# The first strip of a decoder trunk: order of loads, transposes by pairs of blocks, order of splits, six idle products

## The chip, the cores and the metric

The kernel runs on one core of a Trainium2 chip. The metric is the device time of one execution in microseconds (us). The kernel before takes 2492.08 us (median of 3 runs, 2491.33 to 2492.79). Five engines work side by side, each through its own list of instructions, strictly in the order of that list: PE (TensorE: products and transposes), DVE (VectorE), ACT (ScalarE), POOL (GpSimd) and SP (SyncE), which here does nothing but issue DMAs. ACT and POOL issue some DMAs too. An instruction that waits for another engine or for a DMA holds up everything behind it in its own list.

## The reference, cut to what matters

```python
for i in range(DEPTH):                                   # DEPTH = 2, x is 256 x 2048, f32
    h = rms_norm(x, pre_mix_gain[i])
    m = hybrid_mixer(h, positions, w_in[i], ...)         # proj = h @ w_in, then heads, then @ w_out
    x = x + rms_norm(m, post_mix_gain[i])
    h = rms_norm(x, pre_ffn_gain[i])
    f = (silu(h @ w_ffn_gate[i]) * (h @ w_ffn_up[i])) @ w_ffn_down[i]
    x = x + rms_norm(f, post_ffn_gain[i])
    gate = sigmoid(rms_norm(x, ple_gain[i]) @ w_ple_gate[i])
    x = x + (p[i] @ w_ple_proj[i]) * gate
```

Only the very first product is touched: 512 columns of `h @ w_in[0]`, those of the keys and values. `rope` turns the keys afterwards with tables of cosines and sines, which the kernel works out once, at its start.

## The kernel before, in words

**Products.** Every f32 matrix product is made of three products of rounded parts: a factor is split into a high part (`fp32r`, a rounding copy on ACT) and a low part (the rest, a subtraction on DVE), and PE adds high x high, low x high and high x low. `part` (L225 to L234) issues these three for 128 rows of the weight and one token tile of 128 tokens.

**Strips.** `strip` computes 512 output columns for both token tiles, in 8 chunks of 256 weight rows. For each chunk `load_w` (L209) fetches 256 x 512 weights into a tile `wr` (a ring of 4, so a fetch waits until the low split four chunks earlier has read its buffer), makes the high part `wh` on ACT (L173) and the low part `wl` on DVE (L174); `wh` and `wl` are rings of 8, so a split waits until PE has done the chunk eight before. A chunk is 12 products on PE: 2 blocks of 128 rows x 2 token tiles x 3.

**The left factor.** x comes in as eight tiles of 128 tokens x 512 columns, `xr[t][c]`. PE needs it turned, so each 128x128 block is transposed (L188, with `ident`) into a PSUM tile `ms`; then it is multiplied with the norm's gain and split into two `ck` tiles, high and low. In the first strip of all, `load_x` (the argument `pre`) does this between the chunks. For the first 512 columns (`wide`) a token tile's four blocks are multiplied at once on DVE into a tile `nat` (L180), and then split by ACT (L173) and DVE (L174). For the other 1536 columns each block is done by itself: ACT multiplies and rounds (L199), then DVE multiplies and subtracts (L200).

**What sets the order.** The program is written in the order of the Python code, but a scheduler of the framework lists each engine's instructions; `tc.high_priority()` lets a part go ahead, and `behind(names)` keeps the instructions inside it after those that `marks` names. Behind the first strip the order is the same as in a normal strip.

**Other work at the start.** Five idle products of `ident` (L123, `WARM`), one transpose of the first gain rows (L125), `square_sum` of x on ACT (L169), and from the fifth chunk on `constants()`: five small DMAs of gain rows issued by ACT (L136, L138), their transposes on PE (L140, L141) and copies on DVE (L142, L143), and some fifty small DVE instructions, most of them for `rope`'s angles (L361 to L393), which end in the tables `rot` (L438). When the first strip is done, `done_kv` takes its result: DVE multiplies it with the tables (L447), POOL adds and subtracts the halves (L454), and seven chunks later in PE's list the rotated keys are transposed (L466).

Of the kernel before, what the change touches and what calls it, by code (L numbers as in the profile page):

```python
# [46 lines left out]
def decoder(ctx: ExitStack, tc: tile.TileContext, x, p, positions, w_in, attn_sinks,  # L47
# [54 lines left out]
    def nat(shape=(P, W), dt=F32):  # L102
        return np_.tile(list(shape), dt, tag="nat", name="nat")
# [18 lines left out]
    for i in range(WARM):  # L122
        T.matmul(busy[:, 0:P], ident, ident, start=True, stop=True)  # L123
    ps = bank()
    T.transpose(ps[:, 0:32], g0rows, ident[0:32, 0:32])  # L125
    S.preload_act_table(AF.Copy)
# [47 lines left out]
        v = V.tensor_tensor(lo, src, hi.bitcast(F32), op=ALU.subtract)  # L174
        return a, v

    def split_wide(ps, gcols, h, lo):

        g = nat((P, 4, P))
        V.tensor_tensor(g, ps, gcols.unsqueeze(2).to_broadcast([P, 4, P]), op=ALU.mult)  # L180
        marks["x"], _ = split(g, h, lo)

    def split_T(src_blocks, gcols, hl, t, kt0=0, wide=False):
# [10 lines left out]
        if wide:  # L194
            split_wide(ps, gcols, h, lo)
            return
        for b in range(n):
            g = gcols[:, b:b + 1]
            marks["x"] = S.activation(h[:, b], ps[:, b], AF.Copy, scale=g)  # L199
# [6 lines left out]
    def blocks4(a):  # L206
        return [a[:, b * P:(b + 1) * P] for b in range(4)]

    def load_w(w, c, col):  # L209

        raw = wpr.tile([P, 2, W], F32, tag="wr", name="wr")
        nc.sync.dma_start(raw, w[c * 2 * P:(c + 1) * 2 * P, col:col + W].rearrange(
            "(k p) n -> p k n", p=P))
        hi = wps.tile([P, 2, W], F32R, tag="wh", name="wh")
        lo = wps.tile([P, 2, W], F32R, tag="wl", name="wl")
        marks["hi"], marks["lo"] = split(raw, hi, lo)
        return hi, lo

    def strip(lhs, w, col, done, nch=8, row0=0, skew=0, psum=None, pre=None):

        ps = psum or [pacc.tile([P, W], F32, tag="acc", name=f"acc{t}") for t in range(NT)]
        ws = {}

        def part(t, c, lows=(0, 1)):
            hi, lo = ws[c]  # L225
            for k in range(2):
                kt = 2 * c + k
                xh, xl = (a[:, kt % 4, t * P:(t + 1) * P] for a in lhs[kt // 4])
                first, last = kt == 0, kt == 2 * nch - 1
                if 0 in lows:  # L230
                    T.matmul(ps[t], xh, hi[:, k], start=first, stop=False)  # L231
                    T.matmul(ps[t], xl, hi[:, k], start=False, stop=False)  # L232
                if 1 in lows:
                    marks[t, c] = T.matmul(ps[t], xh, lo[:, k], start=False, stop=last)  # L234

        for i in range(nch + skew):
            if pre:
                pre(i)
# [35 lines left out]
        later(wait, lambda: turn((0, 1)))  # L274
        later(wait + 1, lambda: turn((2, 3)))

    def next_in(t, c, xT, gcols, wide=False):
        split_T(blocks4(xr[t][c]), gcols[:, 4 * c:4 * c + 4], xT[c], t, wide=wide)

    def new_ss(name):  # L280
        return [sm.tile([P, 4], F32, name=f"{name}{t}") for t in range(NT)]
# [115 lines left out]
    ss = new_ss("ssx")  # L397
    xT = [new_ck() for c in range(4)]

    def load_x(i):  # L400
        if i % 2 == 0:
            c = i // 2
            for t in range(NT):
                nc.sync.dma_start(xr[t][c], x[0, t * P:(t + 1) * P, c * W:(c + 1) * W])
            with tc.high_priority(), behind((1, i - 2)) if c else nullcontext():
                for t in range(NT):
                    next_in(t, c, xT, gain_cols(0, 0, 16), wide=c == 0)

            def squares():
                with behind("x", "hi"):  # L410
                    for t in range(NT):
                        square_sum(xr[t][c], ss[t][:, c:c + 1])
            later(1 if c == 3 else 2, squares)
        if i == 0:
            def tables():
                with behind((1, 3), "hi", "lo"):
                    constants()
            later(4, tables)

    for l in range(DEPTH):  # L420

# [459 lines left out]
```

## Time and profile before

| | |
|---|---|
| runs, median of 3 | 2492.08 us (2491.33 to 2492.79) |
| profiled execution | 2494.41 us, of which its span (first to last instruction) is 2492.4 us |
| PE busy | 2473.4 us, 99% of the span |
| DVE busy | 1433.2 us, 58% |
| ACT busy | 1177.6 us, 47% |
| chain that ended last | PE 95%, DVE 1%, DMA 1%, ACT 1% |

The shares are over the whole program, which is almost all strips in their steady form. The change concerns its first 60 us, so what counts is who waits for whom there. A matmul's shown duration includes the run through the array; what one costs in a row of them is the distance of two starts.

### The profile page before, as it was taken

How to read it: one execution, taken by the hardware profiler on the slowest of the kernel's cores; microseconds unless marked ns; L12 is line 12 of the kernel's file. 1: busy time of each engine (PE TensorE's matmuls, PEld its weight loads, DVE VectorE, ACT ScalarE, POOL GpSimd, SP SyncE). 2: the span in 40 equal slices, each digit the busy share in tenths (PEclk: the TensorE clock that was granted, in tenths of full speed). 3: DMA queues.
4: the chain of work that ended last, by engine and by line, in shares of the span. 5: the costliest groups of instructions: out<-in, count | busy, mean ns of one | idle time of the engine just before them, and what ended most of it. 6: DMA issues, size and time to landing. Idle time of an engine off the chain costs nothing.

```text
span 2492.4 us, 30948 instructions
## 1 busy us (share of the span) xinstructions
PE 2473.4 (99%) x11725; PEld 2049.2 (82%) x11725; DVE 1433.2 (58%) x1805; ACT 1177.6 (47%) x1676; POOL 96.3 (4%) x209
## 2 busy tenths in 40 slices
PE   8999999999999999999999999999999999999999
PEld 7888887888888888887888888878888888888877
DVE  7676656544554455457567756565445545554574
ACT  6644346444434434446556443464444344344462
POOL 3100001000000000001010000010000000000010
PEclk9999999999999999999999999999999999999999
DMA  8445465666666666665564454656666666666653
GB/s 263 137 139 165 144 193 159 215 191 190 192 188 194 188 193 194 189 200 157 186 204 134 136 173 140 199 170 197 191 190 187 193 193 189 192 190 195 200 169 129
DMA packets 234260, 451.43 MB, mean 181 GB/s; under 512 B 14176, under 2 KB 15104, under 8 KB 234112
## 3 DMA queue, kind: packets, MB, share of 16 engines
q1 hardware_dynamic: 233808, 449.37, 59.3%
q8 instruction: 92, 1.51, 0.3%
q14 instruction: 56, 0.46, 0.1%
q10 hardware_dynamic: 240, 0.07, 0.0%
q0 software_dynamic: 64, 0.02, 0.0%
HBM read 447.31 MB, written 2.10 MB: 180 GB/s over the span
## 4 chain that ended last, share of the span: by engine, by line
PE 95%; DVE 1%; DMA 1%; ACT 1%; issue 0%; POOL 0%; SPq 0%; ACTq 0%; DVEq 0%; POOLq 0%
PE acc L231 29%; PE acc L234 29%; PE acc L232 29%; PE ms L188 2%; DMA wr<-in_w_in_dram 1%; PE ms L661 1%; PE ms L561 1%; DVE wl L174 1%; PE ms L510 0%; ACT wh L173 0%; PE ms L639 0%; ACT junk L169 0%; PE ms L676 0%; PE ms L231 0%; PE ms L234 0%
## 5 line engine op out<-in xcount | busy, mean ns | idle before, releaser
L174 DVE TENSOR_TENSOR wl<-wr,wh 128x1024 fp32r<-128x1024 f32 x840 | 1029.0, 1226 | 960.0 <-ACT wh L173 948.5
L173 ACT CAST wh<-wr 128x1024 fp32r<-128x1024 f32 x840 | 883.4, 1053 | 1158.6 <-PE acc L232 1105.4
L231 PE MATMUL acc<-wh,ck 128*128 128x512 f32 x3328 | 1310.2, 394 | 7.9 <-ACT ck L199 5.6
L232 PE MATMUL acc<-wh,ck 128*128 128x512 f32 x3328 | 1298.6, 390 | 0.9 <-DVE ck L200 0.8
L234 PE MATMUL acc<-wl,ck 128*128 128x512 f32 x3328 | 1299.3, 391 | 0.0
L231 PEld LDWEIGHTS acc<-wh,ck 128*128 128x128 f32 x3328 | 625.6, 188 | 138.4 <-ACT ck L199 10.5
L232 PEld LDWEIGHTS acc<-wh,ck 128*128 128x128 f32 x3328 | 626.2, 188 | 130.8 <-DVE ck L200 4.4
L234 PEld LDWEIGHTS acc<-wl,ck 128*128 128x128 f32 x3328 | 625.6, 188 | 130.7
L199 ACT ACTIVATE ck<-ms,gT 128x128 fp32r<-128x128 f32 x248 | 79.3, 369 | 36.6 <-DVE ck L200 28.6
L200 DVE SCALAR_TENSOR_TENSOR ck<-ms,gT,ck 128x128 fp32r<-128x128 f32 x248 | 76.0, 346 | 21.8 <-ACT ck L199 21.0
L159 POOL TENSOR_TENSOR tiny<-ssf 128x1 f32<-128x1 f32 x4 | 2.1, 536 | 1379.0 <-ACT junk L169 1378.7
L779 ACT ACTIVATE nat<-acc,ry 128x512 f32<-128x512 f32 x44 | 30.2, 686 | 10.7 <-PE acc L234 10.7
L805 DVE TENSOR_TENSOR macc<-acc,macc 128x512 f32<-128x512 f32 x48 | 33.0, 688 | 0.7
L169 ACT ACTIVATE junk<-x 128x512 f32<-128x512 f32 x48 | 30.3, 631 | 6.4 <-DVE x L266 4.1
L785 DVE SCALAR_TENSOR_TENSOR nat<-acc,ry,nat 128x512 f32<-128x512 f32 x44 | 32.4, 748 | 0.1
L661 PEld LDWEIGHTS ms<-q,k 128*128 128x128 f32 x256 | 30.7, 191 | 1.7 <-PE acc L232 0.8
L661 PE MATMUL ms<-q,k 128*128 128x64 f32 x256 | 30.5, 272 | 0.0
L174 DVE TENSOR_TENSOR ck<-ms,ck 128x512 fp32r<-128x512 f32 x44 | 30.1, 684 | 0.0
L188 PE MATMUL ms<-ident,x 128*128 128x128 f32 x192 | 27.8, 281 | 2.1 <-DVE x L838 1.4
L188 PEld LDWEIGHTS ms<-ident,x 128*128 128x128 f32 x192 | 22.8, 144 | 8.5 <-DVE x L838 2.6
L188 PEld LDWEIGHTS ms<-ident,nat 128*128 128x128 f32 x184 | 22.7, 139 | 6.4 <-DVE ck L200 0.4
L188 PE MATMUL ms<-ident,nat 128*128 128x128 f32 x184 | 28.0, 272 | 0.0
(187 smaller groups left out, 861.9 us busy)
## 6 DMA issues: line engine op xcount, KB each, us to landing
wr<-in_w_in_dram SPq DMA_DIRECT2D x176, 512.0 KB, 3.8
wr<-in_w_ffn_gate_dram SPq DMA_DIRECT2D x176, 512.0 KB, 3.7
wr<-in_w_ffn_up_dram SPq DMA_DIRECT2D x176, 512.0 KB, 3.7
wr<-in_w_ffn_down_dram SPq DMA_DIRECT2D x176, 512.0 KB, 3.7
wr<-in_w_out_dram SPq DMA_DIRECT2D x64, 512.0 KB, 4.2
wr<-in_w_ple_gate_dram SPq DMA_DIRECT2D x64, 512.0 KB, 4.3
wr<-in_w_ple_proj_dram SPq DMA_DIRECT2D x8, 512.0 KB, 4.1
x<-in_x_dram SPq DMA_DIRECT2D x8, 256.0 KB, 6.8
```

Source lines behind the costliest of these rows:

```text
L169: S.activation(j[:, 0:shape[1]], src, AF.Square, accum_out=acc)
L173: a = S.copy(hi, src)
L174: v = V.tensor_tensor(lo, src, hi.bitcast(F32), op=ALU.subtract)
L188: T.transpose(ps[:, b], blk, ident)
L199: marks["x"] = S.activation(h[:, b], ps[:, b], AF.Copy, scale=g)
L200: V.scalar_tensor_tensor(lo[:, b], ps[:, b], g, h[:, b].bitcast(F32), op0=ALU.mult, op1=ALU.subtract)
L231: T.matmul(ps[t], xh, hi[:, k], start=first, stop=False)
L232: T.matmul(ps[t], xl, hi[:, k], start=False, stop=False)
L234: marks[t, c] = T.matmul(ps[t], xh, lo[:, k], start=False, stop=last)
L661: T.matmul(pl[:, t * 4 + h].rearrange("p (b k) -> p b k", k=k), s.k[:, h, t * P:(t + 1) * P], up, start=True, stop=True)
L785: V.scalar_tensor_tensor(gate[t], ps, rx2(t)[:, 0:1], gate[t], op0=ALU.mult, op1=ALU.mult)
L805: V.tensor_tensor(m, ps, m, op=ALU.add)
```

## The change

x is loaded in the order of use: the first 512 columns in two halves of 256 for both token tiles, with the first weight chunk between the halves; the next weight chunks are fetched inside `load_x` too, one after each 512 columns of x (`raws`). x is turned by `split_pair`: two blocks of both token tiles into one PSUM tile, one multiplication with the gain for the 128x512 elements, one high and one low split, for all 2048 columns; one such pair belongs to each chunk. The first chunk's high weight split stands ahead of the first pair's work on ACT. Each chunk's weight splits stand behind the splits of its own pair, and the next pairs behind the chunk before. Six idle products (`HOLD`) stand behind the first pair's transposes. The squares are taken one chunk after their pair.

```diff
+HOLD = 6
+    def idle_products(n):
+        for i in range(n):
+            T.matmul(busy[:, 0:P], ident, ident, start=True, stop=True)
+    idle_products(WARM)
...
+    def split_pair(kt, hl, gcols):
+        ps = bank((P, 2, NT, P))
+        for b in range(2):
+            for t in range(NT):
+                c, at = divmod((kt + b) * P, W)
+                marks["turned", kt] = T.transpose(ps[:, b, t], xr[t][c][:, at:at + P], ident)
+        g = nat((P, 2, SEQ))
+        V.tensor_tensor(g, ps.rearrange("p b t n -> p b (t n)"),
+                        gcols[:, kt:kt + 2].unsqueeze(2).to_broadcast([P, 2, SEQ]), op=ALU.mult)
+        k = slice(kt % 4, kt % 4 + 2)
+        marks["xh", kt], marks["xl", kt] = split(g, hl[0][:, k], hl[1][:, k])
...
-                with behind("x") if pre and i == 0 else nullcontext():
-                    ws[i] = load_w(w, row0 // (2 * P) + i, col)
+                with behind(("xh", 2 * i), ("xl", 2 * i)) if pre else nullcontext():
+                    ws[i] = load_w(w, row0 // (2 * P) + i, col, *ready)
...
     def load_x(i):
-        if i % 2 == 0:
-            c = i // 2
-            for t in range(NT):
-                nc.sync.dma_start(xr[t][c], x[0, t * P:(t + 1) * P, c * W:(c + 1) * W])
-            with tc.high_priority(), behind((1, i - 2)) if c else nullcontext():
-                for t in range(NT):
-                    next_in(t, c, xT, gain_cols(0, 0, 16), wide=c == 0)
+        def cols(a, n):
+            c, at = divmod(a, W)
+            for t in range(NT):
+                nc.sync.dma_start(xr[t][c][:, at:at + n], x[0, t * P:(t + 1) * P, a:a + n])
+        def pair(n):
+            split_pair(2 * n, xT[n // 2], gain_cols(0, 0, 16))
+        if i == 0:
+            for c in range(4):
+                if c == 0:
+                    cols(0, 256)
+                    raws[0] = fetch_w(w_in[0], 0, 1024)
+                    cols(256, 256)
+                else:
+                    cols(c * W, W)
+                if c < 3:
+                    raws[c + 1] = fetch_w(w_in[0], c + 1, 1024)
+            with tc.high_priority():
+                hi = high(raws[0])
+                with behind("hi"):
+                    pair(0)
+                with behind(("turned", 0)):
+                    idle_products(HOLD)
+        pairs = {0: (1,), 1: (2, 3)}.get(i, (i + 2,))
+        with tc.high_priority(), behind((1, i - 1)) if i else nullcontext():
+            for n in pairs:
+                if n < 8:
+                    pair(n)
```

PE's list at the program's start, before. `x00_82` and `x10_86` are the first 512 columns of the two token tiles, `ms` PSUM tiles, `acc0` and `acc1` the strip's sums, `DMAHW1` and `DMAHW2` the arrival of the two x tiles.

```order
L123 MATMUL ms_100<-ident_90 128x128 x4
L125 MATMUL ms_106<-ident_90,g0rows_97 128x32 [waits DMAHW0_49]
L188 MATMUL ms_155<-ident_90,x00_82 128x128 [waits DMAHW1_49]
L188 MATMUL ms_155<-ident_90,x00_82 128x128 x3
L188 MATMUL ms_164<-ident_90,x10_86 128x128 [waits DMAHW2_49]
L188 MATMUL ms_164<-ident_90,x10_86 128x128 x3
L231 MATMUL acc0_151<-wh_175,ck_133 128x512 [waits Activation_49]
```

The same place now. `ms_173` is the first pair and `ms_188` the second; `DMAHW1` and `DMAHW2` are the first halves of the two x tiles, `DMAHW4` and `DMAHW5` the second halves, which are issued behind the first weight chunk (`DMAHW3`).

```order
L129 MATMUL ms_106<-ident_90,g0rows_97 128x32 [waits DMAHW0_49]
L187 MATMUL ms_173<-ident_90,x00_82 128x128 [waits DMAHW1_49]
L187 MATMUL ms_188<-ident_90,x00_82 128x128 [waits DMAHW4_49]
L187 MATMUL ms_188<-ident_90,x10_86 128x128 [waits DMAHW5_49]
L187 MATMUL ms_173<-ident_90,x10_86 128x128 [waits DMAHW2_49]
L187 MATMUL ms_188<-ident_90,x00_82 128x128
L187 MATMUL ms_173<-ident_90,x00_82 128x128
L187 MATMUL ms_188<-ident_90,x10_86 128x128
L187 MATMUL ms_173<-ident_90,x10_86 128x128
L126 MATMUL ms_100<-ident_90 128x128 x6
L250 MATMUL acc0_151<-wh_171,ck_133 128x512 [waits Activation_49]
```

The two pairs' transposes now alternate, and the second transpose in the list waits for the second half of an x tile; the six idle products and the strip's first product stand behind all eight.

ACT's list where the small DMAs of gain rows stand (`grows`, `lrows`), before:

```order
L199 ACTIVATE ck_135<-ms_215,gT_99 128x128 [waits PE_49]
L199 ACTIVATE ck_135<-ms_228,gT_99 128x128 [waits PE_49]
L136 DMA grows_110<-in_pre_ffn_gain_dram 32x128 [waits DMAHW2_49]
L136 DMA grows_110<-in_ple_gain_dram 32x128 [waits DMAHW3_49]
L136 DMA grows_110<-in_attn_out_gain_dram 16x128 [waits DMAHW4_49]
```

And now (`nat_254` and `nat_283` are the fifth and the sixth pair, `wh_422` the fifth chunk's high part):

```order
L173 ACTIVATE junk_276,ssx1_132<-x11_87 128x512 [waits DMAHW0_49,Activation_49]
L177 CAST ck_137<-nat_254 128x512 [waits DVE_49]
L140 DMA grows_110<-in_pre_ffn_gain_dram 32x128
L140 DMA grows_110<-in_ple_gain_dram 32x128 [waits DMAHW6_49]
L140 DMA grows_110<-in_attn_out_gain_dram 16x128 [waits DMAHW7_49]
L140 DMA grows_110<-in_hgrn_out_gain_dram 16x128 [waits DMAHW0_49]
L142 DMA lrows_111<-in_hgrn_lb_logits_dram 16x128 [waits DMAHW1_49]
L177 CAST ck_137<-nat_283 128x512 [waits DVE_49]
L225 CAST wh_422<-wr_420 128x1024
```

The five issues stood among the second 512 columns' activations; now they stand together behind the fifth pair's high split, and ahead of the sixth pair's and of the fifth chunk's weight split.

DVE's list around the copies of those rows (L146, L147), now; `wl_424` and `wl_455` are the fifth and the sixth chunk's low parts, `nat_416` the seventh pair.

```order
L178 TENSOR_TENSOR ck_138<-nat_283,ck_137 128x512 [waits Activation_49]
L235 TENSOR_TENSOR wl_424<-wr_420,wh_422 128x1024 [waits DMAHW1_49,Activation_49]
L189 TENSOR_TENSOR nat_416<-ms_411,gT_99 128x512 [waits PE_49]
L146 COPY gT_99<-ms_308 128x96 [waits PE_49]
L147 COPY lbl_112<-ms_308 128x16
L235 TENSOR_TENSOR wl_455<-wr_451,wh_453 128x1024 [waits DMAHW2_49,Activation_49]
```

Before, seven low splits stood ahead of the first of these copies; now five do. From there to the rotation of the keys (L447 before, L495 now) the same low splits and small instructions follow, in other places among each other: in both lists the rotation stands behind the 21st low split, and PE's transposes of the keys stand behind 180 products. Behind that place all lists read alike.

## Rows read from the trace of the kernel before

**Rows 1.** Waits of PE, 0 to 75 us: total us, times, longest.

```profile
PE acc L231 <- ACT wh L173: 2.4, 1, 2.4
PE acc L231 <- ACT ck L199: 1.7, 4, 0.7
PE ms L123 <- POOL ident masks.py:199: 1.6, 1, 1.6
PE ms L466 <- POOL nat L454: 1.3, 1, 1.3
```

**Rows 2.** Chain that ended last, 50 to 75 us: start us, us, what.

```profile
55.38 1.23 DVE wl L174
56.60 0.40 DVE rot L438 x3
57.00 0.72 DVE nat L447 x2
57.78 1.94 POOL nat L454 x2
59.77 0.44 PE ms L466 x2
60.20 0.23 PE acc L231
```

**Rows 3.** Timeline, 0 to 15 us: start us, us, engine, what, [idle before].

```profile
1.56 2.50 PE L123 MATMUL ms<-ident 128*128 128x128 f32 x10 [1.56 <-POOL ident masks.py:199]
4.24 1.97 PE L188 MATMUL ms<-ident,x 128*128 128x128 f32 x8
5.39 0.69 DVE L180 TENSOR_TENSOR nat<-ms,gT 128x512 f32<-128x512 f32 x1 [0.85 <-PE ms L188]
7.49 1.99 ACT L173 CAST wh<-wr 128x1024 fp32r<-128x1024 f32 x2
8.58 0.80 PE L231 MATMUL acc<-wh,ck 128*128 128x512 f32 x1 [2.38 <-ACT wh L173]
9.60 0.63 PE L231 MATMUL acc<-wh,ck 128*128 128x512 f32 x1
10.03 0.63 PE L232 MATMUL acc<-wh,ck 128*128 128x512 f32 x1
13.85 1.04 PE L188 MATMUL ms<-ident,x 128*128 128x128 f32 x8
14.64 0.47 PE L231 MATMUL acc<-wh,ck 128*128 128x512 f32 x1
```

**Rows 4.** DMA issues in 0.7:1.2, 1.2:1.68, 1.68:2.1 and 2.6:3.15, last column us to landing.

```profile
x<-in_x_dram SPq DMA_DIRECT2D x1, 256.0 KB, 2.8
x<-in_x_dram SPq DMA_DIRECT2D x1, 256.0 KB, 3.5
wr<-in_w_in_dram SPq DMA_DIRECT2D x1, 512.0 KB, 5.3
x<-in_x_dram SPq DMA_DIRECT2D x1, 256.0 KB, 6.3
```

**Rows 5.** Timeline of SP's issues and ACT's, 0 to 20 us.

```profile
0.79 0.86 SPq L404 DMA_DIRECT2D x<-in_x_dram  x2
1.70 0.94 SPq L212 DMA_DIRECT2D wr<-in_w_in_dram  x2
15.29 0.43 ACTq L136 DMA_DIRECT2D grows<-in_ple_gain_dram  x1
19.09 0.32 ACTq L138 DMA_DIRECT2D lrows<-in_hgrn_lb_logits_dram  x1
```

**Rows 6.** Busy by stretch: us, PE (x), PEld, DVE, ACT, POOL, granted clock, DMA share, GB/s.

```profile
8.60:14.00 5.40, 5.40 (x14) 4.15 (x15) 3.61 (x4) 4.10 (x7) 0.16 (x6) 1.00 1.03 378
5.39:26.60 21.21, 17.89 (x75) 14.02 (x74) 14.43 (x24) 14.88 (x30) 4.18 (x40) 1.00 0.88 310
26.60:57.70 31.10, 30.37 (x135) 23.86 (x134) 27.14 (x79) 21.81 (x39) 6.36 (x8) 1.00 0.81 253
```

**Rows 7.** Groups by form on DVE, 5.3 to 57.8 us: xcount | busy us, mean ns | idle before.

```profile
L174 DVE TENSOR_TENSOR wl<-wr,wh 128x1024 fp32r<-128x1024 f32 x22 | 26.7, 1220 | 5.1 <-ACT wh L173 5.1
L200 DVE SCALAR_TENSOR_TENSOR ck<-ms,gT,ck 128x128 fp32r<-128x128 f32 x24 | 7.3, 345 | 4.9 <-ACT ck L199 4.8
L180 DVE TENSOR_TENSOR nat<-ms,gT 128x512 f32<-128x512 f32 x2 | 1.4, 692 | 1.0 <-PE ms L188 1.0
L174 DVE TENSOR_TENSOR ck<-nat,ck 128x512 fp32r<-128x512 f32 x2 | 1.4, 686 | 0.1
```

**Rows 8.** Timeline of PE, 57 to 60.6 us.

```profile
57.66 0.39 PE L231 MATMUL acc<-wh,ck 128*128 128x512 f32 x1
57.89 0.39 PE L232 MATMUL acc<-wh,ck 128*128 128x512 f32 x1
58.11 0.39 PE L234 MATMUL acc<-wl,ck 128*128 128x512 f32 x1
59.77 0.44 PE L466 MATMUL ms<-ident,nat 128*128 128x128 f32 x2 [1.26 <-POOL nat L454]
```

**Rows 9.** DMA issues, 0 to 70 us: KB each, median us to landing.

```profile
wr<-in_w_in_dram SPq DMA_DIRECT2D x29, 512.0 KB, 4.9
g0rows<-in_pre_mix_gain_dram ACTq DMA_DIRECT2D x1, 16.0 KB, 2.5
grows<-in_pre_ffn_gain_dram ACTq DMA_DIRECT2D x1, 16.0 KB, 5.0
grows<-in_hgrn_out_gain_dram ACTq DMA_DIRECT2D x1, 8.0 KB, 4.6
lrows<-in_hgrn_lb_logits_dram ACTq DMA_DIRECT2D x1, 8.0 KB, 4.3
```

**Rows 10.** Timeline of ACT, 6 to 10 us.

```profile
6.11 0.62 ACT L173 CAST ck<-nat 128x512 fp32r<-128x512 f32 x1 [3.59 <-DVE nat L180]
9.38 0.63 ACT L169 ACTIVATE junk<-x 128x512 f32<-128x512 f32 x1
9.91 0.19 ACT L169 ACTIVATION_READ_ACCUMULATOR junk<-x 128x1 f32 x1
```

More of the change, by code (lines that the diff above doesn't have):

```diff
@@ L121, in decoder @@
     busy = bank()
-    for i in range(WARM):
-        T.matmul(busy[:, 0:P], ident, ident, start=True, stop=True)
+    def idle_products(n):
+        for i in range(n):
+            T.matmul(busy[:, 0:P], ident, ident, start=True, stop=True)
+    idle_products(WARM)
     ps = bank()
@@ L175, in split, with split_T @@
         return a, v
[L177 to L183, printed above, removed]
+    def split_pair(kt, hl, gcols):
[9 more added lines that the diff above has]
+        marks["xh", kt], marks["xl", kt] = split(g, hl[0][:, k], hl[1][:, k])
+    def split_T(src_blocks, gcols, hl, t, kt0=0):
         n = len(src_blocks)
@@ L193, in split_T @@
             return
-        if wide:
-            split_wide(ps, gcols, h, lo)
-            return
         for b in range(n):
             g = gcols[:, b:b + 1]
-            marks["x"] = S.activation(h[:, b], ps[:, b], AF.Copy, scale=g)
+            S.activation(h[:, b], ps[:, b], AF.Copy, scale=g)
             V.scalar_tensor_tensor(lo[:, b], ps[:, b], g, h[:, b].bitcast(F32),
@@ L213, in load_w, with high @@
             "(k p) n -> p k n", p=P))
+        return raw
+    def high(raw):
         hi = wps.tile([P, 2, W], F32R, tag="wh", name="wh")
+        marks["hi"] = S.copy(hi, raw)
+        return hi
+    def load_w(w, c, col, raw=None, hi=None):
+        if raw is None:
+            raw = fetch_w(w, c, col)
+        if hi is None:
+            hi = high(raw)
         lo = wps.tile([P, 2, W], F32R, tag="wl", name="wl")
-        marks["hi"], marks["lo"] = split(raw, hi, lo)
+        marks["lo"] = V.tensor_tensor(lo, raw, hi.bitcast(F32), op=ALU.subtract)
         return hi, lo
@@ L236, in strip @@
         for i in range(nch + skew):
-            if pre:
-                pre(i)
+            ready = pre(i) if pre else ()
             if i < nch:
-                with behind("x") if pre and i == 0 else nullcontext():
-                    ws[i] = load_w(w, row0 // (2 * P) + i, col)
+                with behind(("xh", 2 * i), ("xl", 2 * i)) if pre else nullcontext():
+                    ws[i] = load_w(w, row0 // (2 * P) + i, col, *ready)
                 if pre and i == 0:
@@ L275, in post_norm, with next_in @@
         later(wait + 1, lambda: turn((2, 3)))
-    def next_in(t, c, xT, gcols, wide=False):
-        split_T(blocks4(xr[t][c]), gcols[:, 4 * c:4 * c + 4], xT[c], t, wide=wide)
+    def next_in(t, c, xT, gcols):
+        split_T(blocks4(xr[t][c]), gcols[:, 4 * c:4 * c + 4], xT[c], t)
     def new_ss(name):
@@ L398, in decoder, with squares @@
     xT = [new_ck() for c in range(4)]
+    raws = {}
     def load_x(i):
-        if i % 2 == 0:
-            c = i // 2
-            for t in range(NT):
-                nc.sync.dma_start(xr[t][c], x[0, t * P:(t + 1) * P, c * W:(c + 1) * W])
-            with tc.high_priority(), behind((1, i - 2)) if c else nullcontext():
-                for t in range(NT):
-                    next_in(t, c, xT, gain_cols(0, 0, 16), wide=c == 0)
-            def squares():
-                with behind("x", "hi"):
+        def cols(a, n):
[25 more added lines that the diff above has]
+                    pair(n)
+        if i % 2 == 0:
+            def squares(c=i // 2):
+                with behind(("xh", 4 * c + 2)):
                     for t in range(NT):
                         square_sum(xr[t][c], ss[t][:, c:c + 1])
-            later(1 if c == 3 else 2, squares)
+            later(1, squares)
         if i == 0:
@@ L418, in load_x @@
             later(4, tables)
+        if i == 0:
+            return raws[0], hi
+        return (raws[i],) if i in raws else ()
     for l in range(DEPTH):
```

2 lines of the change are left out of this document (1 added, 1 removed).

## The prediction

> **What bounds the kernel now.** The table by engine comes first: PE is busy for 99% of the span, so only a stretch in which PE waits or runs slowly can give something back. PE's waits in the first 75 us come next [rows 1]: after the 1.6 us for `ident` there are 2.4 us for the first high weight part, 1.7 us in four waits for high parts of x, and 1.3 us for the rotated keys. The chain of waits says which of these counts for the end: before 59.77 us it does not run through PE, but through DVE's low splits and rotation, then POOL, into PE's transposes of the keys; behind them it is PE alone [rows 2]. PE stood ready at 58.50 us and waited 1.26 us [rows 8]. So whatever PE gains in the first strip is kept only as far as DVE and POOL deliver the keys earlier. The time to predict is that of this one transpose: 59.77 us before.
>
> The timeline adds a second loss. The first chunk's products start 0.43 us apart (9.60, 10.03), and the eight transposes at 13.85 us pass in 0.79 us, against 1.97 us for the eight at 4.24 [rows 3]; later products start 0.227 us apart [rows 8]. The first 14 us thus run at TensorE's lower level, 1.2 of 2.4 GHz, although the column of the granted clock reads 1.00 there [rows 6]; I go by the spacing. PE had worked without a break from 8.58 us, 5.3 us long, when the pace rose; the stretch from 1.56 to 6.2 us had not raised it.
>
> **Step 1, arrival of x.** Before, the two x tiles land at 0.79+2.8 = 3.6 and at 1.23+3.5 = 4.7 us, and the first weight chunk at 1.70+5.3 = 7.0 us [rows 4, 5]: 256, 512 and 1024 KB in the order of issue. Now the order is half, half, weights, half, half. If bytes arrive as before, the first halves are there at 3.6, the weights by about 5.9, the second halves at 7.0. The lower bound is set by issue: the fifth DMA starts at about 2.7 us, and with the 2.8 us of the first one it lands at 5.5. I take 7.0, because the next x tile before, issued at that same 2.7 us, needed 6.3 us [rows 4].
>
> **Step 2, the first transposes.** PE's list alternates the two pairs, and its third transpose needs a second half. Six transposes are left at 7.0 us; at 1.97/8 = 0.25 us each [rows 3] they end at 8.5 us. Before, all eight ended at 6.2. DVE's first multiplication starts at 8.5 instead of 5.39 [rows 3], 3.1 us later: splitting the load buys nothing, since the first pair waits for the second pair's data.
>
> **Step 3, six idle products.** Ten passes take 2.50 us [rows 3], so twelve take 3.0 at the lower level: PE reaches the first real product at 11.5 us. Its operands are there earlier: two multiplications of 0.69 [rows 7] from 8.5, the first high split of 0.62 [rows 10] at 9.9, the first low split at 10.6. Without the idle products it would start at about 10; before, at 8.58. At the lower level they cost about 1.5 us; what pays for them is an earlier rise of the clock.
>
> **Step 4, the clock.** PE is now unbroken from 7.0 us. Taking the same 5.3 us, the pace rises at 12.3: two products at 0.43, ten at 0.227, chunk done at 11.5+0.8+2.3 = 14.6 us, against 13.85. Bounds: 13.3, if the clock is up before the idle products end and the low split at 10.6 releases the products; 16.7, if all twelve run at 0.43. So the first chunk ends 0.75 us later, not earlier.
>
> **Step 5, DVE's work.** Before, from its first multiplication (5.39) to the end of the rotation's first pair of multiplications (57.70), DVE is busy 14.43+27.14 = 41.6 of 52.3 us, idle 10.7 [rows 6]. The change removes 24 small splits (7.3 us) and the four wide instructions (2.8), and adds eight multiplications and eight low splits of 0.69 each (11.0) [rows 7]: 42.5 us. ACT loses 24 activations and gains six casts of 0.62; it hides behind DVE except where its list holds DVE up. The end is therefore 8.5 + 42.5 + idle = 51.0 + idle, and 6.7 us of idle would give the old time.
>
> **Step 6, DVE's idle time, walked list by list** (weight high split 1.0 and low 1.22, squares 0.7 each [rows 3, 7, 10]). DVE finishes two pairs and two weight chunks at 13.7 and waits for the third pair's transposes, behind the first chunk, until 15.0: 1.3 us. Third chunk's high part, queued behind the pair's: 0.2. Fifth pair's high split on ACT ends at 21.0; five DMA issues of about 0.38 [rows 5] hold ACT until 22.9, so the sixth pair's low split waits 1.0 us and the fifth chunk's weight split 0.4. The seventh pair's transposes stand in PE's list behind the transpose of the gain rows, the last of which is issued at 22.3, the `lrows` at 22.6. They landed in 2.5 us when little else was moving and in 4.3 to 5.0 under full load [rows 9]; between, at 3.5, PE goes on at 25.8 to 26.3, and DVE waits 0.4. Eighth pair: 0.2. Sum 3.5. From the ninth chunk on the ring of four `wr` tiles counts: 4.9 us to land [rows 9], 1.05 for the high and 1.22 for the low part make 7.2 us for four chunks, 1.8 each, where DVE's own work is about 1.6 with the small instructions between: up to 2.4 us over twelve chunks, nothing if loads land faster. I take 2.0, since 4.9 is the median of this stretch. Idle 5.5 us, 5.2 less than before.
>
> **Sum.** The rotation's multiplications end at 51.0+5.5 = 56.5 us instead of 57.7, and the keys' transposes move from 59.77 to 58.6. PE gets there at 26.3 + 132 products x 0.227 + 0.4 for the last four transposes = 56.7, so it still waits, 1.9 us. Behind this place all lists are the same and PE is the bound, so the kernel ends 1.2 us earlier. The profiled execution took 2494.41 us, 2.0 around its span and 2.3 above the median of the runs; the difference is taken from the median: 2492.08 - 1.2 = 2490.9 us.
>
> **Rivals.** (a) The second halves land as early as issue allows, at 5.5: every step to the keys moves by up to 1.5 us, the transposes to 57.1, time 2489.4. For it: the halves are small. Against it: the 6.3 us of rows 4. PE's own arrival at 56.7 ends this gain at 3.0 us, 2489.1, unless the gain rows come sooner as well.
> (b) The clock rises later. The transposes between 7.0 and 8.5 may not help it: before, the work from 1.56 to 6.2, which closes with eight transposes, had not raised it [rows 3]. Counting 5.3 us from the idle products at 8.5, the rise comes at 13.8, five products run at 0.43, and the chunk ends at 15.3; DVE's idle grows by 0.7: 2491.6. The Trainium skill says in "TensorE: Matmul & The Clock Gate", Part 4 (PE-mode transpose), that transpose mode does not count as a busy PE in the same way; by that rule this rival is the forecast, and the trace of before agrees without proving it.
> (c) Slower than before. The gain rows decide: PE's transposes of `grows` and `lrows` now stand ahead of the fifth chunk with DMAs issued 3.5 us later than before (22.6 against 19.09), and DVE's copy of `lrows` is ahead of the sixth low split. Each microsecond of landing over 3.5 is a microsecond of idle on DVE. At 5.0, as in rows 9, idle is 7.0 us: 2492.4. The point is 4.7 us of landing; it is against it that the queue is emptier at 22 us than at 15.
> (d) The change does nothing at all, because the two effects on the keys cancel: 2492.1, within the same band.
>
> **How the numbers follow.** Forecast 0.50, (a) 0.20, (b) 0.12, (c) and worse 0.13, (d) 0.05. The low end is (a) with a gain of 3.3 us, 2488.8; the high end is step 4 at its upper bound (2.1 us more) with half of (c), 2494.2. 0.2%, 5 us, is about what a measurement of this kernel can tell from no change. To be faster than that, the keys would have to be there at 54.8 us: PE alone, with 180 products at 0.227, needs 41 us behind a start at 8.6 and four microseconds for transposes, so all waits and the slow clock would have to vanish: 0.03. Slower than that takes a keys' transpose at 64.8, five microseconds of a stall that no row shows: 0.02. So 0.95 for no difference.
>
> **What would show it right or wrong.** Right: the first real product near 11.5 us, not before 8.58; the first eight transposes done near 8.5; products at 0.43 us until about 12; no waits of PE for high parts of x between 24 and 33 us; instead a wait at the gain rows' transposes near 25 us and a wait of one to three microseconds at the keys. Wrong: transposes of the first pair before 6 us, a pace of 0.227 from the first product on, or PE not waiting at the keys at all; then PE alone sets the time and the gain is three microseconds or more. If the `wr` ring is slower than taken, the keys come after 60 us and the kernel is slower.

## The result, and the profile after

| | before | after |
|---|---|---|
| median of 22 runs each, side by side | 2492.12 us (2490.81 to 2494.10) | 2494.95 us (2493.76 to 2497.49) |
| profiled execution | 2494.41 us | 2494.55 us |
| keys' transposes start, profiled execution | 59.77 us | 59.44 us |

The ratio is 1.0012, with a 95% interval of 1.0006 to 1.0017. The changed kernel is slower, by 2.8 us; the prediction said 1.2 us faster. The two profiled executions differ by 0.1 us only, because that of before happens to lie 2.3 us over its median. A slow stretch in it, far behind the first strip, accounts for some 2 us of this; it is shown in the section on why the prediction was wrong.

The waits of PE come first, 0 to 75 us, as in [rows 1].

```profile
PE ms L514 <- POOL nat L502: 3.9, 1, 3.9
PE ms L187 <- DMA x<-in_x_dram: 1.6, 1, 1.6
...
PE ms L144 <- DMA grows<-in_hgrn_out_gain_dram: 0.4, 1, 0.4
```

The waits for high weight parts and high parts of x are gone, as the change would have it. What they cost has come together in one wait, that for the rotated keys: 3.9 us in place of 1.3. The chain of waits of the same kernel, 50 to 75 us, answers to [rows 2].

```profile
56.67 0.71 DVE nat L495 x2
57.46 1.94 POOL nat L502 x2
59.44 0.69 PE ms L514 x2
60.12 0.43 PE acc L250
...
65.24 0.25 PE acc L253
65.49 0.23 PE acc L250
```

Up to the keys' transposes it is the same chain, 0.33 us earlier. Behind them the pace is another one: the products stand 0.43 us apart until 65.24, where before they stood 0.23 apart at once. The granted clock, the third number from the end in these rows of busy time by stretch, says why (columns as in [rows 6]).

```profile
57.00:59.00 2.00, 0.00 (x0) 0.00 (x0) 2.00 (x6) 1.41 (x3) 1.54 (x2) 0.83 0.86 265
59.00:60.00 1.00, 0.56 (x3) 0.57 (x4) 1.00 (x2) 0.00 (x0) 0.98 (x2) 0.50 0.82 229
60.00:65.00 5.00, 5.00 (x14) 3.87 (x14) 1.75 (x3) 1.12 (x3) 1.94 (x4) 0.50 0.65 213
...
66.00:70.00 4.00, 4.00 (x19) 3.30 (x18) 2.83 (x4) 1.43 (x2) 2.25 (x2) 1.00 0.21 29
8.17:57.42 49.25, 46.90 (x218) 38.56 (x217) 42.16 (x89) 32.56 (x49) 7.15 (x31) 1.00 0.83 272
```

While PE stands idle, from 55.51 to 59.44 us, the clock falls to its lower level, 1.2 of 2.4 GHz, and it comes back only at 65 us. From 60 to 65 PE does 14 matmuls and is busy throughout. The same stretch of the kernel before:

```profile
60.00:65.00 5.00, 5.00 (x25) 4.05 (x24) 3.78 (x6) 2.18 (x4) 3.21 (x5) 1.00 0.74 209
```

PE's share of busy time is 100% in both, and 14 matmuls were done in place of 25. This is why the loss is in no list of waits.

The start of the timeline of after, for [rows 3]; here every engine's row has start, length, engine and line.

```profile
4.24 0.47 PE L187 MATMUL ms<-ident,x 128*128 128x128 f32 x1
6.27 1.86 PE L187 MATMUL ms<-ident,x 128*128 128x128 f32 x7 [1.56 <-DMA x<-in_x_dram]
7.93 2.76 PE L126 MATMUL ms<-ident 128*128 128x128 f32 x12
8.17 1.29 DVE L189 TENSOR_TENSOR nat<-ms,gT 128x512 f32<-128x512 f32 x2 [3.64 <-PE ms L187]
10.35 0.80 PE L250 MATMUL acc<-wh,ck 128*128 128x512 f32 x2
10.98 0.40 PE L251 MATMUL acc<-wh,ck 128*128 128x512 f32 x1
...
13.29 1.03 PE L187 MATMUL ms<-ident,x 128*128 128x128 f32 x8
```

One transpose passes at 4.24, then PE waits for the second halves until 6.27. The first product stands at 10.35 (before: 8.58), but from 10.98 on the pace is 0.24, and the first chunk ends at 13.29, 0.56 us ahead of before.

### The profile page after: what moved, and what is told of

The parts are those of the page before. It is cut to its first block, busy times and chain, and to the rows that moved or that the text cites. A ratio compares the mean times of both kernels' runs of the same rounds, so it can differ in the third digit from the quotient of the medians.

```text
span 2492.7 us, 30957 instructions
## 1 busy us (share of the span) xinstructions
PE 2473.5 (99%) x11737; PEld 2051.2 (82%) x11737; DVE 1433.3 (58%) x1793; ACT 1174.5 (47%) x1658; POOL 96.3 (4%) x209
## 4 chain that ended last, share of the span: by engine, by line
PE 95%; DVE 2%; ACT 1%; DMA 1%; issue 0%; POOL 0%; SPq 0%; ACTq 0%; DVEq 0%; POOLq 0%
PE acc L250 29%; PE acc L251 29%; PE acc L253 29%; PE ms L199 2%; PE ms L709 1%; PE ms L609 1%; DVE wl L235 1%; DMA wr<-in_w_in_dram 1%; PE ms L558 0%; PE ms L687 0%; ACT junk L173 0%; ACT wh L225 0%; PE ms L724 0%; PE ms L250 0%; PE ms L253 0%
## 5 line engine op out<-in xcount | busy, mean ns | idle before, releaser
L207 ACT ACTIVATE ck<-ms,gT 128x128 fp32r<-128x128 f32 x224 | 71.5, 368 | 31.5 <-DVE ck L208 26.7
L208 DVE SCALAR_TENSOR_TENSOR ck<-ms,gT,ck 128x128 fp32r<-128x128 f32 x224 | 68.7, 346 | 15.5 <-ACT ck L207 14.8
L502 POOL TENSOR_TENSOR nat<-nat 128x256 f32<-128x256 f32 (+1 forms) x24 | 22.6, 965 | 119.6 <-DVE nat L495 108.4
L577 ACT ACTIVATE nat<-nat,tiny 128x128 f32<-128x128 f32 x64 | 24.8, 389 | 3.9 <-DVE tiny L574 3.6
```

## The experiments

**Theory 1:** PE reaches the keys' transposes earlier while DVE and POOL deliver the keys hardly earlier; the longer wait lets TensorE's clock fall, and the slow products behind it cost more than the 0.33 us gained. **Theory 2:** the loss is made in the first 15 us. **Theory 3:** a late delivery of the keys costs its own length, and the clock plays no part. Each kernel was timed in 11 runs beside 33 of before, whose median was 2492.41 beside those of points 1 to 3, 2492.28 beside those of points 4, 5 and the first of point 6, and 2492.03 beside the rest. The interval of such a ratio is some 2.2 us wide to either side, so smaller differences of medians are weak evidence by themselves; where one is read below, the traces have to carry the argument.

**1. The wait filled.** Sixteen idle products in front of the keys' transposes. The second edited line puts the other token tile's two transposes behind 12 of the products that follow, where they stood behind 7.

```diff
+                if l == 0 and t == 0:
+                    for i in range(16):
+                        T.matmul(pt[:, 0], ident, ident, start=True, stop=True)
...
-            later(8 - t, turn)
+            later(8 if l == 0 else 8 - t, turn)
```

> The changed kernel with 16 idle products of ident on PE between the 180th product and the keys' transposes; nothing else moves on the other engines. Theory 1 (the 3.93 us wait of PE ahead of the keys' transposes in the changed kernel lets TensorE's clock fall, and the products at 0.43 us apart that follow cost about 2.8 us): the wait shrinks to about 0.4 us or whatever the 16 products leave of it, the granted clock reads 1.00 from 55 to 66 us, the keys' transposes stay at about 59.4, and the time is about 2492.1, 2.8 us under the changed kernel. Theory 2 (the loss is made in the first 15 us, by the second halves of x behind the weights and the idle products): filling this wait changes nothing, 2494.9, or it is longer if the products come late. Theory 3 (only the keys' lateness counts, the clock does not): 2494.9 as well, with the transposes at 59.4.

Measured: 2493.40 us (2492.97 to 2496.40), ratio 1.0006, 0.9997 to 1.0015. PE's waits and its clock by stretch:

```profile
PE ms L517 <- POOL nat L502: 1.4, 1, 1.4
```

```profile
55.10:60.29 5.19, 3.74 (x33) 3.54 (x32) 5.17 (x17) 3.29 (x6) 1.97 (x3) 1.00 0.72 232
60.29:65.00 4.71, 4.71 (x23) 3.92 (x24) 3.76 (x6) 2.14 (x4) 3.13 (x4) 1.00 0.78 230
```

The clock stayed up, with nothing useful added to PE's work. The price can be read from its chain of waits beside that of after above.

```profile
60.29 0.44 PE ms L517 x2
...
63.68 0.23 PE acc L250
```

Twelve products and four transposes take 63.68 - 60.29 = 3.39 us here, and 65.49 - 59.44 = 6.05 in the changed kernel: the fall costs 2.7 us. The time fell by 1.5 and not by 2.8, and the interval of the ratio overlaps with that of the changed kernel; in this execution the keys were 0.85 us later (60.29). Five of the 11 runs lie 1 to 3 us above the other six; whether the 1.4 us that are left of the wait let the clock fall in those cannot be seen, as one run alone is profiled. Theories 2 and 3 gave 2494.9 or more.

**2. The keys' transposes later in PE's list**, behind 204 products in place of 180, in the changed kernel and in the kernel before.

```diff
-            later(8 - t, turn)
+            later((10 if l == 0 else 8) - t, turn)
```

> The changed kernel with the keys' transposes moved in PE's list from behind 180 products to behind 204, so that PE has 24 more products (5.4 us) to do ahead of them. Theory 1 (wait and fall of the clock): PE no longer waits there, the granted clock stays 1.00, and the time loses both the 3.9 us of the wait and the 2.8 us behind it: about 2488.2. Theory 3 (the wait alone, no clock): 2494.9 - 3.9 = 2491.0. Theory 2 (the loss is made in the first 15 us): the gain is the wait at most, and a version of before treated in the same way stays about 2.8 us below this one.

> The kernel before with the keys' transposes behind 204 products in PE's list in place of 180. Its wait of 1.26 us goes, and its clock did not fall there: all theories expect 2492.1 - 1.3 = 2490.8. Against the changed kernel with the same edit: theory 1 wants that one to be about 2.6 us faster than this one (PE reaches this place 3.0 us earlier there, at 55.51 against 58.50), theory 2 wants it slower or the same.

Measured: the changed kernel 2489.64 us (2488.42 to 2490.15), ratio to before 0.9987, 0.9978 to 0.9996; the kernel before with this edit 2491.06 us (2490.03 to 2492.99), 0.9994, 0.9985 to 1.0002. PE's waits in the first, 0 to 75 us:

```profile
PE ms L187 <- DMA x<-in_x_dram: 2.0, 1, 2.0
...
PE ms L144 <- DMA grows<-in_hgrn_out_gain_dram: 0.6, 1, 0.6
PE acc L250 <- ACT vv L509: 0.3, 1, 0.3
```

The wait for the keys is gone, and one line turns 2.8 us of loss into 2.8 us of gain. Of the 6.7 us that theory 1 wanted, 5.3 came: more than the 3.9 of the wait alone. Most of the 1.4 us between has its place in the trace, at the start: in this execution the first chunk ended at 14.48 and not at 13.29, as the second halves of x came 0.44 us later and the clock rose later. The kernel before gained 1.35, as all theories had it. So theory 2 falls: with the wait gone, the changed kernel is the faster one. It is so by 1.4 us, not by the 2.6 expected: in these two profiles its 180th product starts at 56.49 against 57.80, 1.3 us earlier and not 3.0.

**3. The fall made in the kernel before.** Three multiplications by 1.0 on POOL delay its keys.

```diff
+            if l == 0 and t == 0:
+                for i in range(3):
+                    G.tensor_scalar(o[:, 0:256], o[:, 0:256], 1.0, None, op0=ALU.mult)
```

> The kernel before, with three more multiplications by one of 128x256 elements on POOL between the rotation of the first keys and their transposes; the result is the same, only the keys come later, by an estimated 1 us for each from the 0.97 us that POOL takes for one of its two steps of the rotation, so that PE waits 4 to 5 us for them in place of 1.26. Theory 1: the granted clock falls to 0.50 behind the wait as it does in the changed kernel, and the time rises by the delay plus 2 to 3 us: about 2497 to 2498. Theory 3 (a wait costs its own length only): it rises by the delay, to about 2495. If the clock does not fall, theory 1 is wrong or lacks a condition.

Measured: 2497.91 us (2493.66 to 2499.11), ratio 1.0020, 1.0011 to 1.0029. PE's wait, and the clock by stretch:

```profile
PE ms L469 <- POOL nat L463: 4.3, 1, 4.3
```

```profile
64.00:69.00 5.00, 5.00 (x14) 3.85 (x14) 1.83 (x3) 2.11 (x4) 1.59 (x3) 0.50 0.04 16
```

The keys' transposes stand at 63.41, 3.64 us later than in [rows 2]; the median rose by 5.50. The edit also moved the transposes in PE's list, behind 183 products in place of 180, so that 0.7 us of the delay is filled with products that PE would else have done behind it. The interval of the time (2.7 to 7.2 us) would still hold the delay alone; the trace would not: behind the wait PE does 14 matmuls in 5 us, as in the changed kernel. The start of this kernel is that of before, so the fall needs nothing of the change but a wait in this place.

**4. Without the six idle products**, in the changed kernel and in its version with the later transposes.

```diff
-HOLD = 6
+HOLD = 0
```

> The changed kernel without the six idle products behind the first pair's transposes (HOLD = 0). Theory 1 (wait at the keys and fall of the clock): what PE gains or loses in the first 15 us only changes how long it waits for the keys, whose time DVE and POOL set; the keys' transposes stay at 59 to 60.5, the clock falls behind the wait, and the time stays at 2494 to 2495.5. Theory 2 (the loss is made in the first 15 us, a good part of it by these idle products, 1.4 us at the granted pace): about 2493.5 or less, without a change at the keys.

> The changed kernel with the keys' transposes behind 204 products, and without the six idle products. Here PE waits nowhere behind 25 us, so the first 15 us count in full. By the rows of the changed kernel the first product waits for its operands until about 9.9 to 10.0 us in place of 10.35, so 0.4 us are gained; and the rise of the clock, seen at 11 us, comes later if the idle products were what raised it: 5 us behind the first product, as in the kernel before, makes it 15 us, some 18 products at 0.43 in place of 2, 3 us lost. Sum: 2489.6 + 2.6 = 2492. If the transposes had raised the clock already: 2489.2.

Measured: 2496.32 us (2494.84 to 2500.29), ratio 1.0017, 1.0008 to 1.0026, and 2490.31 us (2489.45 to 2492.31), 0.9992, 0.9983 to 1.0001: 1.4 us above the changed kernel, and 0.7 above the version with later transposes, both less than the intervals can tell. PE's timeline of the first:

```profile
10.12 1.22 PE L250 MATMUL acc<-wh,ck 128*128 128x512 f32 x2 [1.43 <-ACT ck L177]
...
15.41 1.37 PE L187 MATMUL ms<-ident,x 128*128 128x128 f32 x8
...
62.37 0.69 PE L514 MATMUL ms<-ident,nat 128*128 128x128 f32 x2 [4.32 <-POOL nat L502]
```

The idle products are not the loss: without them neither kernel is faster. Theory 1 had the keys stay where they were, and in this execution they came at 62.37. The third pair's transposes stand behind the first chunk, at 15.41 in place of 13.29, and DVE's waits for such transposes from 8 to 62 us are 8.6 us, of which 4.2 before its first multiplication, against 6.1 and 3.6 in the changed kernel. That PE's pace in the first chunk reaches the keys by way of DVE is one reading, and not shown. The execution took 2499.00 us, 2.7 above the median of its runs: its second halves of x landed at 6.75 us in place of 6.27, its chain to the keys runs through a weight load of 5.93 us, and its granted clock fell once more, to 0.89 on average from 1650 to 1660 us. In the two profiles with later transposes the first chunk ended at 14.48 with the idle products and at 14.91 without, and POOL's step of the rotation began at 58.95 and 58.93, the same. The second kernel was expected at 2492 if the idle products raise the clock, and 2489.2 if the transposes do; it lies between, so it does not tell which.

**5. The first pair first.** The second pair's transposes behind the first pair's, with the later keys' transposes.

```diff
-        with tc.high_priority(), behind((1, i - 1)) if i else nullcontext():
+        with tc.high_priority(), behind((1, i - 1)) if i else behind(("turned", 0)):
```

> The changed kernel with the keys' transposes behind 204 products, and the second pair's transposes behind the first pair's in PE's list, so that the first pair waits for the first halves of x alone. The first pair's transposes should start at about 3.7 us in place of 6.27, DVE's first multiplication at 5 in place of 8.17, and the second pair's at 6.3. The first product then needs the high weight part (7.0) and the first pair's parts, and the idle products, which stand behind the second pair: about 9.7 to 10. Theory of the order (the alternation of the two pairs costs DVE 3 us and PE little): keys ready about 1.5 to 3 us earlier than in the same kernel with the alternation (60.9), time 2489.0 to 2489.6, since PE, which waits no more for the keys, gains only what the first product gains.

Measured: 2489.15 us (2488.26 to 2491.66), ratio 0.9989, 0.9980 to 0.9997, within 0.5 us of the version with alternating pairs. The profiled execution was the slowest of the 11 (2491.66). In it DVE began at 5.39 us in place of 8.63, and POOL's step of the rotation at 59.44 in place of 58.95: the start was gained and lost again. DVE's waits, 8 to 60 us:

```profile
DVE nat L189 <- PE ms L187: 5.3, 5, 1.9
DVE wl L235 <- ACT wh L225: 5.2, 6, 2.2
```

DVE waits 5.2 us for high weight parts, against 2.4 in the version of point 2. In this execution the weights did not come sooner because DVE was ready sooner; one profile of the slowest run does not show that it is so in the others.

**6. A ring of five wr tiles** in the changed kernel, then with the later transposes, then with the first pair first as well, and in the kernel before with the later transposes.

```diff
-    wpr = ctx.enter_context(tc.tile_pool(name="wpr", bufs=4))
+    wpr = ctx.enter_context(tc.tile_pool(name="wpr", bufs=5))
```

> The changed kernel with a ring of five wr tiles in place of four, so that a fetch waits for the low split five chunks before. If the ring of four holds up DVE from the ninth chunk on (2.0 us of idle taken for it in the prediction), the keys' transposes move from 59.44 to about 57.5, PE waits 2 us in place of 3.9 there, and the clock falls less or not at all: 2490 to 2493. If the transfers themselves are the limit, the keys stay at 59 to 60 and the time at 2494 to 2495.5.

> The changed kernel with the keys' transposes behind 204 products and a ring of five wr tiles. With the transposes moved alone, PE still waited 0.3 us once at the next strip's sums, whose PSUM tiles come free when DVE and ACT have read the keys and values, and in one profile 1.8 us. If the ring holds up DVE, keys and values are read 1 to 2 us earlier, this wait goes in all executions, and the time is 2488.5 to 2489.6, 0 to 1 us under the version with four. Whatever PE gains beyond that can only come from the first 15 us, which this does not touch.

> As before with the first pair's transposes ahead of the second pair's, the transposes of the keys behind 204 products and a ring of five. If with four tiles it was the ring that ate the 2.8 us by which DVE started earlier (DVE then waited 5.2 us for high weight parts in place of 2.4), the rotation now ends 1 to 3 us earlier than with four, PE waits at the next strip's sums no more, and the time is 2488.3 or a little less in all executions. If the transfers themselves were the limit: 2489.2 with the spread of the version with four (2488.3 to 2491.7).

> The kernel before with the keys' transposes behind 204 products and a ring of five wr tiles: what these two edits are worth without the change. PE did not wait behind 14 us in the version with the transposes moved alone, except 1.5 us for high parts of x, so the ring can give it nothing: 2491.0, 1.3 to 2 us above the changed kernel with the same two edits.

| five tiles and | median us | ratio to before, interval |
|---|---|---|
| the change alone | 2490.77 (2489.80 to 2493.36) | 0.9995, 0.9987 to 1.0004 |
| later transposes | 2487.93 (2487.49 to 2490.28) | 0.9986, 0.9977 to 0.9995 |
| later transposes, first pair first | 2487.86 (2487.54 to 2489.78) | 0.9986, 0.9977 to 0.9995 |
| before, later transposes | 2490.65 (2490.03 to 2491.40) | 0.9994, 0.9985 to 1.0003 |

With the change alone, PE's wait for the keys falls into two, and the clock by stretch reads 1.00 throughout:

```profile
PE ms L514 <- POOL nat L502: 2.0, 2, 1.3
```

The keys came at 59.03, only 0.4 us earlier and not the 2 expected, and PE came at 57.74, 2.2 later than in the changed kernel's profile; so this does not show that the ring moves the keys. Half of PE's lateness is the order: with this edit the transposes stand behind 185 products in place of 180, which takes 1.1 us more. It does show a version of the change in which PE waits 2.0 us, the clock does not fall, and 4.2 us are gained.

Not all of that is gained in the first strip. The ring serves every strip, and far behind the first one there is a wait of PE that shrinks with it; first the changed kernel, then the one with five tiles:

```profile
1260.75 0.66 PE L199 MATMUL ms<-ident,x 128*128 128x128 f32 x4 [1.55 <-DVE x L886]
```

```profile
1256.58 0.66 PE L199 MATMUL ms<-ident,x 128*128 128x128 f32 x4 [0.62 <-DVE x L886]
```

This wait is 1.2 to 2.1 us in the nine profiles with a ring of four and 0.6 us in the five with a ring of five. Counting PE's products in both traces, the version with five tiles gains 0.9 us on the changed kernel at this place. With the later transposes it gains 0.7 there, out of the 1.7 between the medians of the two rings. With the first pair first, DVE's wait for high weight parts goes from 5.2 us to 1.8, as if there the ring had held the loads back; the 5.2 are those of the slowest run. Yet the order of the pairs then gives 0.07 us: nothing. The second row of the table beats both kernels, by 4.1 us against before and by 7 against the change. The same two edits without the change leave 2490.65: 2.7 us is what the change is worth where PE never waits for the keys. In these two profiles the 180th product starts at 56.19 against 59.13, 2.9 us apart, about the 3.0 of the first two profiles (55.51 against 58.50 for its end). A part of this may be the clock as well: in the profile of the kernel before with these edits it fell behind two waits for high parts of x, of 0.79 and 0.71 us, which the change takes away.

```profile
27.30:30.70 3.40, 3.40 (x10) 2.66 (x9) 3.07 (x7) 1.87 (x4) 0.00 (x0) 0.50 0.94 323
```

**7. Idle products in PE's wait for the second halves of x**, ahead of the second pair's transposes, in the version with five tiles, later transposes and the first pair first.

```diff
...
-                    idle_products(HOLD)
+                    marks["idle"] = idle_products(HOLD)
...
-        with tc.high_priority(), behind((1, i - 1)) if i else behind(("turned", 0)):
+        with tc.high_priority(), behind((1, i - 1)) if i else behind("idle"):
```

> The version before this one (first pair first, transposes of the keys behind 204 products, ring of five) with the six idle products between the first pair's transposes and the second pair's, where PE waits 1.4 us for the second halves of x anyway. They then lie in that wait (12 passes of 0.23 us take 2.8 us, so they reach 1.3 us beyond it): the second pair's transposes start at about 8.0, the first product follows them at about 9.0 in place of 10.2. A gain of 1 us if TensorE's clock rises as early as it does now (products at 0.23 from 10.8); a loss of up to 1 us if it rises by as much later. I expect 2487.5 to 2488.5.

Measured: 2488.77 us (2487.32 to 2492.07), ratio 0.9987, 0.9978 to 0.9995. PE's timeline:

```profile
5.14 1.92 PE L126 MATMUL ms<-ident 128*128 128x128 f32 x12
...
7.97 0.73 PE L251 MATMUL acc<-wh,ck 128*128 128x512 f32 x2 [0.34 <-ACT ck L178]
...
11.47 1.04 PE L188 MATMUL ms<-ident,x 128*128 128x128 f32 x8
...
24.46 0.28 PE L145 MATMUL ms<-ident,grows 96*128 96x96 f32 x1 [2.73 <-DMA grows<-in_hgrn_out_gain_dram]
```

The start gained more than expected, the first chunk ending at 11.47, 3.3 us ahead of the version without (14.77). Half of this was given back at the gain rows: PE waits 2.7 us for them, against 1.1 without, and starts their transposes at 24.46 against 26.10. ACT issues the last of the four `grows` loads at 19.59 against 21.52, 1.9 us earlier and not 3.3. The 1.6 us that are left are seen between these two executions, the second fastest of one version and the second slowest of the other. The medians do not show them: that of this version is 0.9 us above the one without, outside the 2487.5 to 2488.5 expected, and its runs spread over 4.8 us. Why is open.

## Why the prediction was wrong

**Which bound sets the end** was read rightly. The chain to the keys runs through DVE and POOL, and it was put 1.2 us earlier; it came 0.33 earlier, because DVE's idle time (step 6) was put too low.

**Step 1, arrivals:** 7.0 us predicted for the second halves, 6.27 measured; other executions had up to 6.75 with the same list. **Step 2:** 8.5 predicted for the first eight transposes, 8.13 measured. That the first pair waits for the second pair's data is so; that this matters is not (point 5).

**Steps 3 and 4, idle products and clock:** the first product at 10.35 instead of 11.5, full pace from 10.98 instead of 12.3, the first chunk done at 13.29 instead of 14.6. So PE came to the keys at 55.51 instead of 56.7. Rival (b), a later rise, fell in this profile; three other profiles with the same list had the chunk done at 14.3 to 14.5, so the early rise is in part luck. The Trainium skill's rule in "TensorE: Matmul & The Clock Gate", Part 4 (PE-mode transpose), that transposes do not count like products, is neither shown nor refuted: in each of these runs a wait, idle products or products stand beside the transposes.

**Step 5, DVE's work:** 42.5 predicted, 42.16 measured. **Step 6, DVE's idle:** 5.5 predicted, 49.25 - 42.16 = 7.1 measured, so the rotation's multiplications end at 57.42 instead of 56.5. DVE's waits, 8 to 60 us, the first row with 3.6 us that lie before 8.17:

```profile
DVE nat L189 <- PE ms L187: 6.1, 5, 3.6
DVE wl L235 <- ACT wh L225: 3.1, 5, 1.3
```

Rival (c), the gain rows, cost PE 0.4 us at 3.8 us of landing; it decided nothing here, and only came into force when the start was made faster (point 7).

**The step that failed is the Sum:** "it still waits, 1.9 us. Behind this place all lists are the same and PE is the bound, so the kernel ends 1.2 us earlier." The lists are the same, and the pace is not. PE's earliness was taken to be worth nothing, as hidden behind the wait for the keys. It was worth less than nothing: with PE 1.2 us earlier than forecast and the keys 0.8 later, the wait was 3.9 us in place of 1.9, and the clock fell. By the rows, -0.33 for the keys and +2.7 for twelve products and four transposes at the lower level give +2.3. Counted product by product, the two profiles say the same: the 180th starts 3.0 us earlier in the changed kernel, and the 204th 2.3 us later, at 67.85 against 65.55. By the medians it is +2.8; the other 0.5 is not accounted for and is within the spread of either kernel's runs. That the fall causes the loss is shown from both sides, by taking it away with idle work (point 1) and by making it in the kernel before (point 3). No rival of the prediction has this term. The high end of its range, 2494.2, is also not what its own terms give: 2490.9, 2.1 for step 4 and half of the 1.5 of (c) make 2493.7, and the 3.3 us of the low end go beyond the 3.0 at which (a) says that the gain ends.

The trace of before had such a fall in it, at a place outside the first 60 us. PE's timeline there:

```profile
1649.24 0.39 PE L234 MATMUL acc<-wl,ck 128*128 128x512 f32 x1
1651.50 0.50 PE L231 MATMUL acc<-wh,ck 128*128 128x512 f32 x1 [1.87 <-ACT ck L199]
...
1653.07 0.63 PE L232 MATMUL acc<-wh,ck 128*128 128x512 f32 x1
1653.49 0.63 PE L234 MATMUL acc<-wl,ck 128*128 128x512 f32 x1
...
1656.10 0.40 PE L231 MATMUL acc<-wh,ck 128*128 128x512 f32 x1
...
1666.29 0.39 PE L232 MATMUL acc<-wh,ck 128*128 128x512 f32 x1
```

A wait of 1.87 us, then products 0.42 us apart, then 0.23 again; the granted clock of 1650 to 1660 is 0.83. The profile of after has full clock there, and here are its records of the first and the last of these products:

```profile
1651.64 0.40 PE L253 MATMUL acc<-wl,ck 128*128 128x512 f32 x1
...
1666.63 0.39 PE L251 MATMUL acc<-wh,ck 128*128 128x512 f32 x1
```

The changed kernel is 2.4 us behind at the first and 0.3 at the last. So this one execution of before lost 2.1 us there that the one of after did not lose, partly in a longer wait (1.87 against 1.02 us) and partly in the slow products, and a comparison of the two spans did not show the loss. The prediction said that it forecast a wait of 1.9 us at the keys, beside a trace in which a wait of 1.9 us had just this consequence. The Trainium skill describes the like in "TensorE: Matmul & The Clock Gate", Part 1 (HAM oscillation): waits for DMAs between bursts of products throw the clock back, and each next burst begins slowly. The trace agrees for the wait of 3.9 us, with a granted clock of 0.50 from 59 to 65 us; the waits of that example last some 3 to 5 us, so it would not have warned of one of 1.9.

## What to carry to other kernels

An engine that waits is not free to come earlier: if it is TensorE, price the longer wait with the products behind it at the lower level, here 2.7 us for a wait that grew from 1.3 to 3.9. It is not the price of every fall: here the slow products ran until 65 us, in the profile of point 5 they began at 61.9 and ended before 65. When a change speeds up one side of a meeting place, move the meeting place in the same change, here the transposes by 24 products. A busy share of 100% says nothing on the clock: count matmuls per stretch, and search the whole trace of before for falls of the granted clock, which show what a wait can cost and also which executions are no fair base. And when an edit is meant for one place, look at PE's list and at its waits everywhere: two of the edits here moved the transposes by some products as well, and the ring of five also worked at 1257 us.

## What the runs showed of the hardware

The length of a wait alone did not tell whether the clock falls behind it. It fell within waits of 3.93, 4.26 and 4.32 us for the keys, and behind 1.87 us at 1650 in before, 2.05 us at 1654 in the kernel without idle products, and the two of 0.79 and 0.71 us in point 6. In the profile of point 5 it fell about 1.5 us behind a wait of 1.77 us, while PE was at work again:

```profile
59.98 0.50 PE L250 MATMUL acc<-wh,ck 128*128 128x512 f32 x1 [1.77 <-ACT vv L509]
60.32 0.40 PE L251 MATMUL acc<-wh,ck 128*128 128x512 f32 x1
...
62.52 0.63 PE L251 MATMUL acc<-wh,ck 128*128 128x512 f32 x1
```

It did not fall behind 2.73 us at the gain rows in point 7, where the stretch from 26 to 28 us has a clock of 1.00, nor behind 2.07 us at 1257 in the kernel of point 1, where that from 1256 to 1262 has 1.00. Nor does the start repeat itself: with the same list of instructions up to there, the first chunk ended at 13.29, 12.97, 14.48, 14.30 and 14.53 us in five profiles. In all of them the column of the granted clock reads 1.00 from the beginning, while the spacing of the products shows the lower level; there the spacing is to be read, and later on both agree.
